# Loading the last image pair of a dilated convolution in ten pieces

## The chip, the cores and the metric

The kernel runs on one core of a Trainium2 chip. A core has five engines with their own instruction streams: PE multiplies matrices, DVE, ACT and POOL work elementwise, and SP only issues transfers here. Data move between device memory and the on-chip buffer by 16 DMA engines, which all the issuing engines share. The metric is the device time of one launch in microseconds (us). Before the change the median of three runs is 126.34 us, with 126.18 and 126.83 as the lowest and the highest.

## The reference

A 3x3 convolution with dilation 2 over 16 images of 64 channels and 64x64 pixels, with 128 output channels, zero padding, all in f32:

```python
x_pad = np.pad(x, ((0, 0), (0, 0), (pad, pad), (pad, pad)), mode='constant')
for b, co, ci, kh, kw in ...:
    output[b, co] += weight[co, ci, kh, kw] * x_pad[b, ci, kh*2:kh*2+h, kw*2:kw*2+w]
```

The input is 16.8 MB and the output 33.6 MB, so most of what moves is output.

## The kernel before

Images are taken in eight pairs. The two images' 64 channels each fill the 128 partitions of a tile `x16[pb]` (f16, 128 x 64 rows x 64 columns), so partition p below 64 is channel p of the first image, and the others are the second image. Pair 0 is loaded as f32 by SP (L75) and cast on chip. Pairs 1 to 7 are loaded by `load` (L81), issued by POOL, with the cast from f32 to f16 done on the way; each such load was one transfer of 128 partitions with 64 rows, 2 MB read and 1 MB written.

For each pair, POOL adds rows two apart into a tile `s16[pb]` (`prepare`, L141), in two parts, rows 0 to 36 and rows 36 to 64. PE then computes, for each of four row groups u of a pair, three accumulations in PSUM (`phase`, L186): one on the sums and two on differences of weights, on the even and the odd rows. ACT copies the first from PSUM (L204), DVE adds it to the other two and writes the output tile `o` (L209). The tile `o` has three buffers (128 partitions, 2 images, 64 rows, f32, 4 MB), so pair pb writes into the one whose store was issued for pair pb - 3.

The order is written out by hand; each engine executes its instructions in the order of the program. Loads of pairs 1 to 4 are issued at the beginning. The load of pair pb + 2 is issued by POOL in group u = 1 of pair pb, ahead of `prepare(pb + 1, 0, 36)` (L195 to L199); the load of pair 7 so stands in pair 5. There are six buffers for `x16`. Stores are issued by SP when a pair's last addition is done (L221): one of 4 MB for pairs 0 to 4, two of 2 MB for pairs 5 and 6 (L224), and four of 1 MB for pair 7, two after half of its rows.

Every transfer signals a semaphore when it has landed. Transfers issued by POOL use eight semaphores in turn, and those of SP another eight. An issue that comes to a semaphore again first waits until the transfer that used it before has landed.

Of the kernel before, what the change touches and what calls it, by code (L numbers as in the profile page):

```python
# [10 lines left out]
def kernel(  # L11
# [7 lines left out]
    nc = tc.nc  # L19

    B, CI, H, W = x.shape
# [5 lines left out]
    P = 128  # L27
    f32 = mybir.dt.float32
    f16 = mybir.dt.float16
    NP = B // 2  # L30
# [18 lines left out]
    wpool = ctx.enter_context(tc.tile_pool(name="wpool", bufs=1))  # L49
    x16pool = ctx.enter_context(tc.tile_pool(name="x16pool", bufs=6))  # L50
# [9 lines left out]
    x_pair = x.rearrange("(nb two) c h w -> nb (two c) h w", two=2)  # L60
# [5 lines left out]
    x16 = {}  # L66
# [11 lines left out]
    def load(pb, cuts):  # L78
        x16[pb] = x16pool.tile([P, H, W], f16, tag="x16", name=f"x16_{pb}")
        for lo, hi in zip(cuts, cuts[1:]):  # L80
            nc.gpsimd.dma_start(out=x16[pb][:, lo:hi], in_=x_pair[pb, :, lo:hi])  # L81

    AHEAD = 5

# [15 lines left out]
    for name, a in (("w21", 2), ("w01", 0)):  # L100
        for u in range(2):
            eng = nc.vector if name == "w21" else nc.gpsimd
            eng.tensor_sub(  # L103
                out=w16[:, SLOT[name] * KW : (SLOT[name] + 1) * KW, u, :],
                in0=w32k[:, a * KW : (a + 1) * KW, :],
                in1=w32k[:, KW : 2 * KW, :],
            )

            if name == "w01" and u == 0:
                load(1, [0, H])  # L110

    w_sb = wpool.tile([P, NS * KW, CO], f16, name="w_sb")
    for n, name in enumerate(("w1", "w21", "w0", "w01", "w2")):
        ps = cpool.tile([P, 2, NB], f32, tag="ps", name=f"wt{n}")
        k0 = SLOT[name] * KW
        for j in range(KW):
            nc.tensor.matmul(  # L117
                out=ps[:, 0, j * CO : (j + 1) * CO],
# [16 lines left out]
    def prepare(pb, lo, hi):  # L135
        if pb not in s16:
            s16[pb] = sumpool.tile([P, 2 * NQ, W], f16, tag="s16", name=f"s16_{pb}")
        src = (x16[pb] if pb else x32).rearrange("p (q e r) w -> p q e (r w)", e=2, r=2)
        dst = s16[pb].rearrange("p (q r) w -> p q (r w)", r=2)
        q0, q1 = lo // 4, hi // 4  # L140
        nc.gpsimd.tensor_add(  # L141
            out=dst[:, q0:q1], in0=src[:, q0:q1, 0, :], in1=src[:, q0:q1, 1, :]
        )

    prepare(0, 0, 20)
    for pb in range(2, AHEAD):
        load(pb, [0, H])
# [33 lines left out]
    def phase(pb, u, terms):  # L181

        ps = cpool.tile([CO, 2, NB], f32, tag="ps", name="ps")
        for pair in zip(*(conv(pb, hb, ps[:, hb], u, terms) for hb in range(2))):
            for m in pair:
                nc.tensor.matmul(**m)  # L186
        return ps

    BOTH = NP - 3
    for pb in range(NP):  # L190
        o = opool.tile([P, 2, H, W], f32, tag="o", name=f"o{pb}")
        ov = o.rearrange("p b (q e r) w -> p b q e (r w)", e=2, r=2)
        for u in range(NU):

            if u == 1 and AHEAD <= pb + 2 < NP:  # L195
                load(pb + 2, [0, H])
            if pb + 1 < NP:
                if u == 1:
                    prepare(pb + 1, 0, 36)  # L199
                elif u == 2:  # L200
                    prepare(pb + 1, 36, H)

            s32 = spool.tile([P, 2, NB], f32, tag="s32", name="s32")
            nc.scalar.copy(out=s32, in_=phase(pb, u, [("w1", 2, 0)]))  # L204
            for e, terms in enumerate(
                ([("w21", 1, 0), ("w0", 1, -1)], [("w01", 0, 0), ("w2", 0, 1)])
            ):
                ps = phase(pb, u, terms)
                nc.vector.tensor_add(  # L209
                    out=ov[:, :, u * UQ : (u + 1) * UQ, e, :],  # L210
                    in0=ps.rearrange("p b (q c) -> p b q c", c=QW),
                    in1=s32.rearrange("p b (q c) -> p b q c", c=QW),
                )

            step = NU // 2 if pb == NP - 1 else NU
            if (u + 1) % step == 0:
                fl = slice((u + 1 - step) * 4 * UQ, (u + 1) * 4 * UQ)
                if pb < BOTH:  # L220
                    nc.sync.dma_start(out=out_pair[pb], in_=o)  # L221
                else:
                    for hb in range(2):
                        nc.sync.dma_start(out=out[2 * pb + hb, :, fl], in_=o[:, hb, fl])  # L224
# [35 lines left out]
```

## Time and profile before

| | |
|---|---|
| median of three runs | 126.34 us (126.18 to 126.83) |
| span of the profiled execution, first to last instruction | 124.3 us |
| own time of the profiled execution | not listed apart from the span; the runs' median lies 2.0 us above the span |
| PE busy | 105.2 us (85%) |
| DVE busy | 80.8 us (65%) |
| ACT busy | 39.6 us (32%) |
| POOL busy | 41.4 us (33%) |
| DMA: queue of SP (q1) | 2944 packets, 35.95 MB, 68.9% of 16 engines' span |
| DMA: queue of POOL (q0) | 1008 packets, 7.34 MB, 28.4% of 16 engines' span |
| granted TensorE clock | 0.965 of full speed on the mean |

Shares are of the span. The megabytes are those written; POOL's loads read twice as many. A DMA share is the time that packets took, as a share of 16 engines. An average over the span hides that stages differ, so the slices and windows are read beside it: they give the busy time of each engine in each stretch. PE's time is modelled; a busy PE need not be PE at its peak.

### The profile page before, as it was taken

How to read it: one execution, taken by the hardware profiler on the slowest of the kernel's cores; microseconds unless marked ns; L12 is line 12 of the kernel's file. 1: busy time of each engine (PE TensorE's matmuls, PEld its weight loads, DVE VectorE, ACT ScalarE, POOL GpSimd, SP SyncE). 2: the span in 40 equal slices, each digit the busy share in tenths (PEclk: the TensorE clock that was granted, in tenths of full speed). 3: DMA queues.
4: the chain of work that ended last, by engine and by line, in shares of the span. 5: the costliest groups of instructions: out<-in, count | busy, mean ns of one | idle time of the engine just before them, and what ended most of it. 6: DMA issues, size and time to landing. Idle time of an engine off the chain costs nothing.

```text
span 124.3 us, 2244 instructions
## 1 busy us (share of the span) xinstructions
PE 105.2 (85%) x981; PEld 55.7 (45%) x981; DVE 80.8 (65%) x71; ACT 39.6 (32%) x40; POOL 41.4 (33%) x33
## 2 busy tenths in 40 slices
PE   6357999999999999999999999999999999960000
PEld 2043555555555555555555555555555555520000
DVE  0470199787778777877769778777877787770000
ACT  4760823333333333333333333333332433320000
POOL 2859998794095009500930093000000000000000
PEclk9999999999999999999999999999999999999655
DMA  4999999999999999999999999999999999999991
GB/s 129 346 359 218 214 214 216 224 237 411 393 327 314 332 306 319 316 390 314 324 345 427 425 427 432 422 427 427 432 438 427 432 414 432 427 417 419 422 406 71
DMA packets 3961, 43.42 MB, mean 349 GB/s; under 512 B 368, under 2 KB 368, under 8 KB 624
## 3 DMA queue, kind: packets, MB, share of 16 engines
q1 hardware_dynamic: 2944, 35.95, 68.9%
q0 software_dynamic: 1008, 7.34, 28.4%
q8 instruction: 7, 0.11, 0.3%
q14 instruction: 2, 0.02, 0.0%
HBM read 17.07 MB, written 33.55 MB: 407 GB/s over the span
## 4 chain that ended last, share of the span: by engine, by line
PE 80%; DMA 5%; POOL 2%; DVE 1%; DVEq 1%; SPq 0%; issue 0%
PE ps L186 80%; DMA x<-in_x_dram 5%; POOL s L141 2%; DVE o L209 1%; DVEq L255 1%; SPq L64 0%; DVEq L209 0%
## 5 line engine op out<-in xcount | busy, mean ns | idle before, releaser
L209 DVE TENSOR_TENSOR o<-ps,s 128x1024 f32<-128x1024 f32 x64 | 76.7, 1223 | 25.9 <-PE ps L186 16.8
L186 PE MATMUL ps<-x,w_sb 64*128 64x496 f16 (+3 forms) x768 | 85.3, 368 | 0.0
L186 PEld LDWEIGHTS <-w_sb 64*128 64x128 f16 x960 | 53.4, 95 | 49.3 <-issue 3.7
L204 ACT COPY s<-ps 128x1024 f32<-128x1024 f32 x32 | 32.4, 1012 | 63.0 <-PE ps L186 63.0
L141 POOL TENSOR_TENSOR s<-x 128x1152 f16<-128x1152 f16 (+4 forms) x18 | 35.1, 1971 | 31.1 <-PE ps L186 28.3
L186 PE MATMUL ps<-s,w_sb 64*128 64x496 f16 (+1 forms) x192 | 26.5, 379 | 2.1 <-POOL s L141 2.1
L81 POOL DMA_DIRECT2D x<-in_x_dram x7 | 4.0, 579 | 0.0
L132 ACT CAST x<-x 128x1024 f16<-128x1024 f32 (+1 forms) x3 | 2.8, 973 | 3.4 <-DMA x<-in_x_dram 3.4
L93 PE MATMUL warm<-zero 128*128 128x512 f16 x6 | 2.7, 630 | 1.2 <-DVE zero L87 1.2
L117 PE MATMUL wt<-ident,w 128*128 128x128 f16 x15 | 1.8, 312 | 2.1 <-ACT w L99 2.1
L103 DVE TENSOR_TENSOR w<-w 128x192 f16<-128x192 f32 x2 | 1.5, 800 | 2.5 <-DMA w<-in_weight_dram 2.5
L117 PEld LDWEIGHTS <-w 128*128 128x128 f16 x15 | 1.5, 146 | 3.0 <-ACT w L99 3.0
L99 ACT CAST w<-w 128x576 f16<-128x576 f32 x2 | 2.3, 1222 | 1.6 <-DMA w<-in_weight_dram 1.6
L103 POOL TENSOR_TENSOR w<-w 128x192 f16<-128x192 f32 x2 | 1.9, 951 | 2.4 <-DMA w<-in_weight_dram 2.4
L126 DVE CAST w_sb<-wt 128x384 f16<-128x384 f32 x3 | 1.6, 552 | 1.4 <-PE wt L117 1.4
L93 PEld LDWEIGHTS <-zero 128*128 128x128 f16 x6 | 0.7, 138 | 2.3 <-DVE zero L87 1.2
L99 ACT ACT_TABLE_LOAD x1 | 1.3, 1283 | 0.7 <-PEq L241 0.7
L128 ACT CAST w_sb<-wt 128x384 f16<-128x384 f32 x2 | 1.0, 478 | 1.1 <-PE wt L117 1.1
L130 DVE CAST x<-x 128x1280 f16<-128x1280 f32 x1 | 0.8, 826 | 0.5 <-DMA x<-in_x_dram 0.5
L87 DVE MEMSET zero<- 128x256 uint32 x1 | 0.3, 272 | 0.9 <-PEq L241 0.9
masks.py:199 POOL TENSOR_SCALAR_AFFINE_SELECT ident<-ident 128x128 f16<-128x128 f16 x1 | 0.3, 292 | 0.1
masks.py:197 POOL MEMSET ident<- 128x128 f16 x1 | 0.2, 204 | 0.3 <-POOLq L241 0.3
(4 smaller groups left out, 0.4 us busy)
## 6 DMA issues: line engine op xcount, KB each, us to landing
out_dram<-o SPq DMA_DIRECT2D x5, 4096.0 KB, 21.6
out_dram<-o SPq DMA_DIRECT2D x4, 2048.0 KB, 12.4
x<-in_x_dram POOLq DMA_DIRECT2D x7, 1024.0 KB, 16.0
out_dram<-o SPq DMA_DIRECT2D x4, 1024.0 KB, 10.6
x<-in_x_dram SPq DMA_DIRECT2D x1, 1152.0 KB, 6.5
x<-in_x_dram SPq DMA_DIRECT2D x1, 896.0 KB, 10.6
w<-in_weight_dram SPq DMA_DIRECT2D x1, 288.0 KB, 2.9
```

Of the source, the lines that this page charges most:

```text
L81: nc.gpsimd.dma_start(out=x16[pb][:, lo:hi], in_=x_pair[pb, :, lo:hi])
L93: nc.tensor.matmul(out=warm[:, 0], lhsT=zero[:, 0:P], rhs=zero, start=True, stop=True)
L99: nc.scalar.copy(out=w16[:, 0:NK, u, :], in_=w32k)
L103: eng.tensor_sub(out=w16[:, SLOT[name] * KW : (SLOT[name] + 1) * KW, u, :], in0=w32k[:, a * KW : (a + 1) * KW, :], in1=w32k[:, KW : 2 * KW ...
L117: nc.tensor.matmul(out=ps[:, 0, j * CO : (j + 1) * CO], lhsT=w16[:, k0 + j, :, :].rearrange("o t i -> o (t i)"), rhs=ident, start=True, st ...
L126: nc.vector.tensor_copy(out=dst, in_=ps[:, 0, 0 : KW * CO])
L132: nc.scalar.copy(out=x16[0][:, lo:hi], in_=x32[:, lo:hi])
L141: nc.gpsimd.tensor_add(out=dst[:, q0:q1], in0=src[:, q0:q1, 0, :], in1=src[:, q0:q1, 1, :])
L186: nc.tensor.matmul(**m)
L204: nc.scalar.copy(out=s32, in_=phase(pb, u, [("w1", 2, 0)]))
L209: nc.vector.tensor_add(out=ov[:, :, u * UQ : (u + 1) * UQ, e, :], in0=ps.rearrange("p b (q c) -> p b q c", c=QW), in1=s32.rearrange("p b ( ...
L255: with _tile.TileContext(nc) as tc:
```

## The change

The load of pair 7 is replaced by a function of its own, which issues ten loads in place of one: partitions 0 to 111 with all 64 rows; partitions 112 to 127 with rows 0 to 37; and rows 38 to 63 of these 16 partitions by eight loads of two partitions each. After them two small reads are issued, of three partitions with one row and of four partitions with two rows, into tiles of their own that nothing else reads. The other pairs are loaded as before. The rows and values that arrive in `x16[7]` are the same.

```diff
+    def load_uneven(pb):
+        x16[pb] = x16pool.tile([P, H, W], f16, tag="x16", name=f"x16_{pb}")
+        cut, p1 = H - 26, P - 16
+        parts = [(0, p1, 0, H), (p1, P, 0, cut)]
+        parts += [(p, p + 2, cut, H) for p in range(p1, P, 2)]
+        for p0, p2, lo, hi in parts:
+            nc.gpsimd.dma_start(
+                out=x16[pb][p0:p2, lo:hi], in_=x_pair[pb, p0:p2, lo:hi]
+            )
+        for n, row in ((3, 0), (4, 1)):
+            side = wpool.tile([P, (1 + row) * W], f32, name=f"side{n}")
+            nc.gpsimd.dma_start(
+                out=side[0:n].rearrange("p (h w) -> p h w", w=W),
+                in_=x_pair[pb, 0:n, 0 : 1 + row],
+            )
...
             if u == 1 and AHEAD <= pb + 2 < NP:
-                load(pb + 2, [0, H])
+                if pb + 3 == NP:
+                    load_uneven(pb + 2)
+                else:
+                    load(pb + 2, [0, H])
```

Further on, "the 112 partitions", "the 16 partitions" and "the two-partition loads" are the ten loads in the order of issue.

## The prediction

> **What bounds the kernel now.** I read the page first, then the time line of Pool, the waits, and last the table of windows, finely cut at the end. The page's slices and queues:
>
> ```profile
> PE   6357999999999999999999999999999999960000
> DMA  4999999999999999999999999999999999999991
> GB/s 129 346 359 218 214 214 216 224 237 411 393 327 314 332 306 319 316 390 314 324 345 427 425 427 432 422 427 427 432 438 427 432 414 432 427 417 419 422 406 71
> DMA packets 3961, 43.42 MB, mean 349 GB/s; under 512 B 368, under 2 KB 368, under 8 KB 624
> q1 hardware_dynamic: 2944, 35.95, 68.9%
> q0 software_dynamic: 1008, 7.34, 28.4%
> ```
>
> PE is full from slice 4 to slice 36, but the last four slices have no matmul and a DMA row still at 9. The DMA row is full from the second slice on. The low rates early are loads: the GB/s counts what is written (f16) while twice as much is read (f32), so 216 GB/s there is the same load on the engines as 430 GB/s of stores. The chain on the page (PE 80%) does not see this; it ends with the last DVE addition, 12 us before the span does. What comes after is only stores, and they were queued already:
>
> ```profile
> SPq L255 <- DMA out_dram<-o: 9.2, 4, 2.4
> DMA to landing us min/median/max: 8.9/9.9/10.9
> ```
>
> The second line is for the two stores issued at 112.0 and 112.4. Each is 1 MB and holds the 16 engines 2.5 us at 427 GB/s; the first landed after 8.9 us, so about 6 us of older stores stood ahead of it, less the way to memory and back. The end is therefore the moment when the slowest of the 16 DMA engines has worked off all that was ever given to it. The windows of the end show that they do not finish together (last two columns: mean share of the 16 that is busy, GB/s):
>
> ```profile
> 119.00:120.00 1.00, 0.00 (x0) 0.00 (x0) 0.00 (x0) 0.00 (x0) 0.00 (x0) 0.50 1.07 451
> 120.50:121.00 0.50, 0.00 (x0) 0.00 (x0) 0.00 (x0) 0.00 (x0) 0.00 (x0) 0.50 0.85 360
> 121.00:121.50 0.50, 0.00 (x0) 0.00 (x0) 0.00 (x0) 0.00 (x0) 0.00 (x0) 0.50 0.66 279
> 121.50:122.00 0.50, 0.00 (x0) 0.00 (x0) 0.00 (x0) 0.00 (x0) 0.00 (x0) 0.50 0.35 147
> 122.00:122.50 0.50, 0.00 (x0) 0.00 (x0) 0.00 (x0) 0.00 (x0) 0.00 (x0) 0.50 0.16 66
> 122.50:123.00 0.50, 0.00 (x0) 0.00 (x0) 0.00 (x0) 0.00 (x0) 0.00 (x0) 0.50 0.04 16
> ```
>
> Times 16, about 14 engines are at work before 121.0, 11 in the next half microsecond, then 6, 3, and under one. So some four engines are done by 121.0 (the earliest a little after 120.5), the other twelve stop one after another between 121.0 and 122.9, with their middle near 121.9. An engine that gets more work than before moves the end as soon as it passes 122.9; work taken from the others can only bring forward what the slowest one had.
>
> **The change part by part.** Everything outside the eighth pair's load keeps its order on all five engines; Pool has 12 DMA issues where it had one.
>
> *Bytes.* All rows of the pair are still read once. The 1008 packets of queue 0 are 7 x (128 + 16): one packet for each partition and one short completion packet for each engine, none cut finer (16 for each of the 23 DMAs also gives the 368 under 512 B). So 112 partitions are 7 packets on each engine, 16 partitions one each, and a load of two partitions is two packets and can lie on two engines at most.
>
> *Price of a packet.* In the windows where loads run alone:
>
> ```profile
> 10.00:15.00 5.00, 5.00 (x36) 2.41 (x36) 0.00 (x0) 2.69 (x3) 5.00 (x7) 1.00 1.02 216
> 15.00:20.00 5.00, 5.00 (x50) 2.73 (x48) 4.72 (x5) 2.02 (x2) 4.49 (x3) 1.00 1.06 221
> 20.00:25.00 5.00, 5.00 (x53) 2.68 (x50) 4.25 (x4) 1.23 (x2) 4.20 (x3) 1.00 1.03 215
> ```
>
> the mean is 217 GB/s, 13.6 for each engine; a partition writes 8192 bytes and so takes 0.604 us, one row of 64 takes 9.4 ns, 26 rows 0.245 us, 38 rows 0.36 us.
>
> *Who gets them.* Before, every engine had 8 x 0.604 = 4.83 us of this load. Now every engine has 7 x 0.604 + 0.36 = 4.59 us, and the sixteen 26-row packets come on top. If each two-partition load is dealt anew from the first engine, as the 128 partitions are, all eight land on the same two engines: these get 4.59 + 8 x 0.245 = 6.55 us (+1.72), the other fourteen lose 0.245. If successive loads go on to the next two engines, the eight cover all sixteen and nothing moves. The trace of before has no load of fewer than 128 partitions, so both are open; the bounds are 0 and +1.72 us on two engines. I take the upper one, because nothing in the trace shows a place that is carried from one load to the next, and every load in it starts evenly.
> On this the Trainium skill (DMA: Bandwidth & Descriptors, section "Why a DMA increments its semaphore by 16 and not by 1") states both: a software-issued copy whose size gives fewer than 16 engines takes consecutive ones from a round-robin cursor, yet some direct copies were measured to be dealt over 16 with ⌈partitions/16⌉ each, which for two partitions means the first two engines. By the first the sum would be +0.2 us, by the second it is the one below; no run here shows it yet.
>
> *Completions and marks.* Eleven more loads are eleven more completion packets on each engine. Their price: stores of 4 MB and more run at 437, 429 and 429 GB/s (70 to 85 us), where a DMA ends every 9.8 us; those of 2 and 1 MB at 426, 413 and 434 (105 to 120 us), where one ends every 2.5 to 4.9 us. The 2% are at most 0.045 us for each end, so 0 to 0.5 us for eleven; I take 0.2 us, since the lower rate also has other gaps in it. The two marked reads (768 and 2048 bytes) are under 20 ns by the rate above.
> The Trainium skill (DMA: Bandwidth & Descriptors) speaks against the change: "Rules for kernel authors" says to coalesce small transfers, and "Anatomy of one DMA" gives each software DMA about 2.0 us of fixed cost. As engine time that would be 11 x 2.0 = 22 us; the three windows above, with loads back to back and the engines busy throughout, do not show it as engine time, so nothing of it is in the sum.
>
> *Pool.* Its time line around the load:
>
> ```profile
> 46.58 4.21 POOL L141 TENSOR_TENSOR s<-x 128x1152 f16<-128x1152 f16 x2 [7.65 <-PE ps L186]
> 50.73 0.57 POOL L81 DMA_DIRECT2D x<-in_x_dram  x1
> 58.95 4.21 POOL L141 TENSOR_TENSOR s<-x 128x1152 f16<-128x1152 f16 x2 [7.65 <-PE ps L186]
> ```
>
> One issue takes 0.58 us on the mean of seven, twelve take 7.0 us, within the 7.65 us that Pool idles. But the software loads use eight semaphores in turn: in Pool's order the sixth two-partition load waits for pair 6's load, and the last two wait until the 112 and the 16 partitions have landed. The whole load landed 16.0 us after its issue, at 66.7; so Pool stands until about 66.5, and behind it `prepare(6)` starts near 68.5 instead of 58.95 and ends near 73. PE reads that sum first at 85.74 (start of pair 6 in PE's time line): 12 us of cover. `prepare(7)` begins at 73 instead of 71.31, its second half at 75.5 with the last small loads landed some 5 us before; PE needs it at 98.1. Cost 0; without that cover, each microsecond past 85.7 would stall PE by one.
>
> *PE, DVE, SP.* The slot of output buffers is reused when a store has landed; DVE waited for that once, 1.2 us. On the two loaded engines stores land up to 1.9 us later, so the next wait may be 1 to 2 us and push PE's end by less. The 6 us of stores queued at 112 hide it: cost 0.
>
> *Sum.* The loaded pair: +1.72 + 0.2 = +1.92 us each; the rest −0.245 + 0.2 = −0.05. If the later of the two stood in the middle of the twelve, 121.9, it ends at 123.8, and the last packet moves from 122.9 to 123.8: +0.9 us. The profiled span is 124.3 and would be 125.2; the median of the runs, 126.34, lies 2.0 us above the span, all outside the DMA tail, so 127.2. Measurement of this kernel (126.18 to 126.83 in three runs) cannot tell much under 0.5%, 0.63 us, from no change.
>
> **The rivals.**
> 1. *Two-partition loads rotate over the engines.* Nothing is moved, only completions are added: 126.34 + 0.2 = 126.5. For it: loads of 128 partitions, all that the trace has, would look the same with a moving start. Against it: no sign of a place kept.
> 2. *The fixed pair is early.* The other side of my forecast: if both engines are among the four that stop by 121.0, they end at 122.5 to 122.9, the rest at 122.85, and the end stays or comes 0.05 us earlier (0.25 if completions cost nothing): 126.1 to 126.4, not slower. It decides at a stop before of 121.0; up to 121.6 the loss stays under 0.63 us. By then about 7 of the 16 have stopped, so two drawn at random are both that early in 7/16 x 6/15 = 0.18 of cases; the first two engines may share a reason for being early, so I give more.
> 3. *Pool jams.* If the small loads' landing takes longer than I think, `prepare(6)` passes 85.7 and PE stalls; with PE late by more than the 6 us of queued stores the end follows. That needs Pool held past 87 us, 20 us more than I find: 128 to 130.
>
> **How the numbers follow.** Fixed pair, later member after 121.6: 0.55, own range 126.9 to 128.3 (a member at 122.9 plus 1.92, rounded up to the bound of completions). Fixed pair, early: 0.25. Rotating: 0.15. Pool: 0.03. Something that frees the slowest engine by over 0.63 us: 0.02; the relief itself cannot, being 0.245 us. The range 126.1 to 128.2 takes in all but the ends. Slower by over 0.5% gets 0.53 of the first case and the third rival, 0.56; within 0.5% the early pair, rotation and the rest of the first case, 0.41; faster 0.03.
>
> **What would show it.** Right: in the windows after 121 us, a share near 0.12 (two of 16) that lasts until the end, after the rest have stopped near where they did; Pool's last DMA issues after 64 us and `prepare(6)` near 68; PE without a wait at pair 6. Wrong: the same staircase as now at the same times (rotation, or an early pair, which a longer 0.85 plateau and a steeper end would tell), a wait of PE for Pool, or a DMA row below 9 before the end.

## The result, and the profile after

The median of six runs is 127.17 us (126.94 to 127.61), that of the kernel before on the same chip 126.19 us (126.14 to 126.83). The ratio is 1.0067, with a 95% interval of 1.0045 to 1.009: slower by 0.67%. The ratios in this document are estimated from all the fast runs, so they need not be the quotient of the two medians, which is 1.0077 here. The profiled execution took 127.02 us with a span of 124.7 us, against 124.3 us before.

The page of the kernel after, the lines that answer to those of before (DMA row by slices, rates, packets, queues), and the row of the new loads with their idle time:

```profile
DMA  4999999999999999999999999999999999999991
GB/s 135 365 349 215 221 210 218 213 252 412 420 302 326 305 310 326 328 418 305 307 333 426 422 419 414 447 426 426 415 436 426 436 407 426 431 423 418 428 384 45
DMA packets 4298, 43.42 MB, mean 348 GB/s; under 512 B 685, under 2 KB 689, under 8 KB 977
q1 hardware_dynamic: 2944, 35.95, 68.8%
q0 software_dynamic: 1344, 7.34, 28.4%
L89 POOL DMA_DIRECT2D x<-in_x_dram x10 | 5.1, 512 | 12.1 <-DMA x<-in_x_dram 12.1
```

The DMA row is as full as before and the same megabytes move; queue 0 has 336 packets more, and their time is still 28.4% of the engines' span. So the DMA engines remain what bounds the kernel. The windows of the end in the kernel after (last two columns: mean share of the 16 engines that is busy, GB/s):

```profile
121.00:121.50 0.50, 0.00 (x0) 0.00 (x0) 0.00 (x0) 0.00 (x0) 0.00 (x0) 0.50 0.62 262
121.50:122.00 0.50, 0.00 (x0) 0.00 (x0) 0.00 (x0) 0.00 (x0) 0.00 (x0) 0.50 0.47 197
122.00:122.50 0.50, 0.00 (x0) 0.00 (x0) 0.00 (x0) 0.00 (x0) 0.00 (x0) 0.50 0.20 82
122.50:123.00 0.50, 0.00 (x0) 0.00 (x0) 0.00 (x0) 0.00 (x0) 0.00 (x0) 0.50 0.12 49
123.00:123.50 0.50, 0.00 (x0) 0.00 (x0) 0.00 (x0) 0.00 (x0) 0.00 (x0) 0.50 0.04 16
```

A window counts a packet where it starts, so the last 0.04 is one packet of 0.31 us. By the packet records it starts at 123.18 and ends at 123.49, where the last packet of before ends at 122.90. Two engines work on past 122.5, and the other one stops at 123.0.

The packet records of the same trace also tell which engines these are, since each packet starts within some 20 ns of the end of the one before on its engine and can be followed. Two engines, and only these, carry nine short packets each of the eighth pair, one of 4864 bytes (38 rows in f16) and eight of 3328 (26 rows). One of the eight takes 266 ns, with 20 ns of overlap with the next: 0.246 us. One of this pair is the engine that stops at 123.5. The other stops by 122.5, though its chain is less certain, as some packets of different engines start within a nanosecond or two of each other. The engine that stops at 123.0 is not of the pair. It is an engine that is slower than the others in every trace: its last landing follows its last packet by 0.47 us, as in before, where it is the last to stop (0.46), while the other engines' last landings follow by 0.31 to 0.37. So the forecast share of 0.12 is there, but only one of the two engines behind it is of the pair, and that one ends at 123.5 and not at 123.8.

Pool's time line in the kernel after, between 45 and 90 us:

```profile
51.23 3.57 POOL L89 DMA_DIRECT2D x<-in_x_dram  x7
55.58 0.51 POOL L89 DMA_DIRECT2D x<-in_x_dram  x1 [0.78 <-DMA x<-in_x_dram]
66.28 0.50 POOL L89 DMA_DIRECT2D x<-in_x_dram  x1 [10.19 <-DMA x<-in_x_dram]
67.88 0.50 POOL L89 DMA_DIRECT2D x<-in_x_dram  x1 [1.10 <-DMA x<-in_x_dram]
69.11 0.51 POOL L94 DMA_DIRECT2D side<-in_x_dram  x1 [0.73 <-DMA x<-in_x_dram]
70.34 0.50 POOL L94 DMA_DIRECT2D side<-in_x_dram  x1 [0.72 <-DMA x<-in_x_dram]
70.86 6.54 POOL L157 TENSOR_TENSOR s<-x 128x1152 f16<-128x1152 f16 x3
78.19 1.88 POOL L157 TENSOR_TENSOR s<-x 128x896 f16<-128x896 f16 x1 [0.80 <-DMA x<-in_x_dram]
```

Seven issues go out at once, the eighth waits for the pair before, and the ninth stands 10.19 us until the 112 partitions have landed. `prepare(6)` starts at 70.86. PE does not feel it; the one wait of PE for Pool in the table of waits is that of the first pair, 2.0 us at the start:

```profile
PE ps L202 <- POOL s L157: 2.0, 1, 2.0
```

What the profile does not hold is more than half of the loss. Each run's time minus its own span is 1.77 us before (median of the 23 runs beside the first experiments; 1.73 to 1.85 over all calls) and 2.29 us after (2.24 to 2.32): +0.52 us outside the span, with no overlap of the two ranges. The median span is 124.9 us against 124.6 to 124.7 in the later calls: about +0.25 us inside it. In the call of the result, where the spans of the kernel before are not on record, the medians differ by 0.98 us, which leaves 0.46 us for the inside. Spans of one kernel differ by 1 us and more from run to run, so the size of the part inside is uncertain. Below, "above the span" means this difference, as a median of the runs.

### The profile page after: what moved, and what is told of

Same layout as the page of the kernel before. It is cut to its first block, busy times and chain, and to the rows that moved or that the text cites. A ratio compares the mean times of both kernels' runs of the same rounds, so it can differ in the third digit from the quotient of the medians.

```text
span 124.7 us, 2261 instructions
## 1 busy us (share of the span) xinstructions
PE 105.8 (85%) x981; PEld 54.8 (44%) x981; DVE 81.1 (65%) x71; ACT 39.5 (32%) x40; POOL 47.0 (38%) x44
## 3 DMA queue, kind: packets, MB, share of 16 engines
q0 software_dynamic: 1344, 7.34, 28.4%
## 4 chain that ended last, share of the span: by engine, by line
PE 81%; DMA 5%; POOL 2%; DVE 1%; DVEq 1%; SPq 0%; issue 0%
PE ps L202 81%; DMA x<-in_x_dram 5%; POOL s L157 2%; DVE o L228 1%; DVEq L274 1%; SPq L64 0%; DVEq L228 0%
## 5 line engine op out<-in xcount | busy, mean ns | idle before, releaser
L202 PE MATMUL ps<-x,w_sb 64*128 64x496 f16 (+3 forms) x768 | 86.4, 372 | 0.0
L89 POOL DMA_DIRECT2D x<-in_x_dram x10 | 5.1, 512 | 12.1 <-DMA x<-in_x_dram 12.1
L81 POOL DMA_DIRECT2D x<-in_x_dram x6 | 3.5, 586 | 0.0
L133 PE MATMUL wt<-ident,w 128*128 128x128 f16 x15 | 1.2, 219 | 2.2 <-ACT w L115 2.1
L133 PEld LDWEIGHTS <-w 128*128 128x128 f16 x15 | 0.9, 97 | 3.2 <-ACT w L115 3.0
L94 POOL DMA_DIRECT2D side<-in_x_dram x2 | 1.0, 502 | 1.5 <-DMA x<-in_x_dram 1.5
```

The lines of the kernel that those rows point to most:

```text
L89: nc.gpsimd.dma_start(out=x16[pb][p0:p2, lo:hi], in_=x_pair[pb, p0:p2, lo:hi])
L133: nc.tensor.matmul(out=ps[:, 0, j * CO : (j + 1) * CO], lhsT=w16[:, k0 + j, :, :].rearrange("o t i -> o (t i)"), rhs=ident, start=True, st ...
```

## The experiments

Each experiment was timed in five rounds beside the kernel before. "Pool's length" is the number of instructions in Pool's program: 55 before, 69 after (each trace holds one fewer).

**One part undone: the same number of loads, evenly dealt (e1_even).** The 26 rows come by eight loads of all 16 partitions with three or four rows each, so the number of loads stays and no pair of engines gets more.

```diff
-        parts += [(p, p + 2, cut, H) for p in range(p1, P, 2)]
+        rows = [cut, 42, 46, 49, 52, 55, 58, 61, H]
+        parts += [(p1, P, lo, hi) for lo, hi in zip(rows, rows[1:])]
```

> As many loads as in the change (ten and the two marked reads), but the last 26 rows of the 16 partitions come by eight loads of 16 partitions with 3 or 4 rows each, so no engine gets more than another. Theory A (two fixed engines carry 1.72 us more, and that sets the end): the loss of 0.98 us (126.19 to 127.17) goes, 126.2 to 126.4, and no pair of engines outlasts the rest. Theory B (the eleven more loads cost it, by their completion packets on every engine or by Pool's late prepare): 127.0 to 127.2.

Measured: 126.94 us against 126.47, ratio 1.0046 (1.0027 to 1.0066). The median span is 124.65 us against 124.7, so nothing is lost inside it; above the span it is 2.28 us, against 1.77 in the kernel before. The eleven further loads thus cost the DMA engines nothing that shows, and taking the pair's load away takes only about 0.25 us of the loss away, which six and twelve runs hardly tell from nothing. The time is near Theory B's, but the span does not hold it: something that both versions share costs 0.5 us outside the span.

**The pair alone, in two doses (e2_side3, e3_side6).** The kernel before, with three and with six whole two-partition reads of 64 rows behind Pool's last addition, where no engine waits for them. Each costs the two engines 0.604 us: +1.81 and +3.62 us.

```diff
                 elif u == 2:
                     prepare(pb + 1, 36, H)
+                elif u == 3 and pb + 2 == NP:
+                    side = wpool.tile([P, H, W], f16, name="side")
+                    for i in range(3):
+                        nc.gpsimd.dma_start(
+                            out=side[2 * i : 2 * i + 2], in_=x_pair[0, 2 * i : 2 * i + 2]
+                        )
```

> The kernel before, with three more loads of two partitions and 64 rows each (data not used), issued by Pool after its last addition. Pool's work and PE's inputs are untouched and only three loads are added. Theory A: 3 x 0.604 = 1.81 us more on two engines, as much as in the change; 127.0 to 127.3. Theory B: 3 of 11 loads' worth or nothing, 126.2 to 126.5.

> As the run with three side loads, but six: 3.62 us more on two engines. Theory A: from the point where the pair sets the end every microsecond on it counts in full, so 1.8 us above the run with three: 128.8 to 129.1. Theory B: twice the small loss of that run at most, under 126.8.

Measured: three reads 126.67 us, ratio 1.0018 (0.999 to 1.0046), median span 124.9 (+0.2), 1.77 us above the span. That is not clear of noise and less than the 127.0 to 127.3 of Theory A. Six reads 128.55 us, ratio 1.0176 (1.0144 to 1.0207), median span 126.4 (+1.7), 2.15 above the span. The windows of the end with six reads:

```profile
123.00:123.50 0.50, 0.00 (x0) 0.00 (x0) 0.00 (x0) 0.00 (x0) 0.00 (x0) 0.50 0.12 49
123.50:124.00 0.50, 0.00 (x0) 0.00 (x0) 0.00 (x0) 0.00 (x0) 0.00 (x0) 0.50 0.15 66
124.00:124.50 0.50, 0.00 (x0) 0.00 (x0) 0.00 (x0) 0.00 (x0) 0.00 (x0) 0.50 0.08 33
124.50:125.00 0.50, 0.00 (x0) 0.00 (x0) 0.00 (x0) 0.00 (x0) 0.00 (x0) 0.50 0.08 33
```

By the packet records the two engines that carry the reads, six each, stop at 124.43 and 125.16, and all others have stopped by 123.22. Two-partition reads all go to the same two engines; if they went round, six of them would have put 0.604 us on each of twelve engines and this tail would not be there. The larger dose also measures where the pair stands without it: 124.43 and 125.16 less 3.62 us are 120.8 and 121.5. In the kernel after, 122.5 and 123.5 less 1.72 us give 120.8 and 121.8. The later of the two thus has about 1.1 to 1.4 us of room to the slowest engine's 122.9, and some 0.3 more in a median run, whose span is that much longer than the traced one; so the first dose hardly shows.

**Many loads of a few bytes (e4_marks).** The kernel before with 14 one-row reads of 2 to 15 partitions in the same place.

```diff
+                elif u == 3 and pb + 2 == NP:
+                    for n in range(2, 16):
+                        side = wpool.tile([P, W], f32, name=f"side{n}")
+                        nc.gpsimd.dma_start(out=side[0:n], in_=x_pair[0, 0:n, 0])
```

> The kernel before, with fourteen reads of one row from 2 to 15 partitions (data not used), issued by Pool after its last addition. The number of marks that an engine's packets carry tells its place among the sixteen, and so where the first two engines end in the kernel before. Theory A: engines 0 and 1 end early enough that the relief does not matter and late enough that 1.72 us more passes the last one: between 121.2 and 122.0 in the profiled span; time 126.2 to 126.4. Theory B (each load costs 0.98/11 us): 14 loads give 127.4.

Measured: 127.38 us, ratio 1.0083 (1.0053 to 1.0114), median span 125.1 (+0.4), 2.28 above the span. This is the time that Theory B named, but most of it has another place: loads with almost no bytes cost the full 0.5 us outside the span again. They also served as marks: since the reads differ in their number of partitions, the packet records tell the engines apart. The engine that ends last (its last packet lands at 124.08, the next engine's at 122.91) carries 11 of the 14 marks, so it is the fifth, number 4 if the first is 0. It is the slow engine of the other traces.

By then the loads themselves were a suspect, and so was Pool's program, which is longer in after, e1, e3 and e4 than before.

**Pool's length without loads, and both at once (e5_pad14, e6_pad6, e7_side3_pad11).** The kernel before with 14, and with 6, memsets of one column behind Pool's last addition, and the three side reads of e2 with 11 memsets.

```diff
+                elif u == 3 and pb + 2 == NP:
+                    for i in range(14):
+                        nc.gpsimd.memset(side[:, i : i + 1], 0.0)
```

> The kernel before, with fourteen one-column memsets on Pool after its last addition: no load is added, Pool's program is as long as in the change (69 instructions, before 55). Theory C (half a microsecond of the change's loss lies outside the profiled span and comes from Pool's longer program): span as before, 124.6, time 0.45 to 0.6 us above the kernel before of this call, and an instruction packet of 8 KB after the end of the span. Theory D (it is the number of software loads that have to be closed): no loss, within 0.1 us.

> As the run with fourteen memsets, but six: Pool's program has 61 instructions, as with the six side loads, whose time lay 2.15 us above its span (before 1.77, the change 2.3). Theory C: 0.3 to 0.45 us above the kernel before, all outside the span. Theory D: within 0.1 us.

> The kernel before with the three side loads of two partitions (1.81 us more on two engines) and eleven memsets on Pool (69 instructions): the two suspected parts of the change's loss without its ten pieces. Theories A and C together: 0.2 us in the span and 0.5 us outside it, 0.7 to 1.0 us above the kernel before, the change's loss. Theory C alone: 0.5. Theory A alone: 0.2.

On Pool's time line in e5 the memsets are nothing, and they end 49 us before the span does:

```profile
74.87 0.54 POOL L205 MEMSET side<- 128x1 f32 x14
```

Measured: e5 127.08 us, ratio 1.0063 (1.0037 to 1.0089); e6 126.76, 1.0044 (1.0015 to 1.0073); e7 126.98, 1.0071 (1.0042 to 1.01). Without one more load or byte, 14 idle instructions cost nearly what the whole change costs. The time above the span is 2.28, 2.18 and 2.30 us, and the median spans (124.8, 124.6 and 124.7 against 124.6) are not clear of noise, so Theory D is out. e7 comes out no slower than e5, so it does not show the 0.2 us that Theory A adds to Theory C. In e5 it is not the end of the DMA work that moves; its windows at 122.0 and at 122.5 are those of before to 0.04:

```profile
122.00:122.50 0.50, 0.00 (x0) 0.00 (x0) 0.00 (x0) 0.00 (x0) 0.00 (x0) 0.50 0.12 49
122.50:123.00 0.50, 0.00 (x0) 0.00 (x0) 0.00 (x0) 0.00 (x0) 0.00 (x0) 0.50 0.04 16
```

**The ten pieces in a short program (e9_short), with its control (e10_before_short).** In e9 the kernel after is cut to 58 Pool instructions: the two marked reads go, the two `prepare` calls of a pair become one, the first pair's are joined into fewer, and Pool's subtraction of the weights (two instructions) moves to DVE. e10 is the kernel before with the same joining and moving, 45 instructions.

```diff
-            eng = nc.vector if name == "w21" else nc.gpsimd
+            eng = nc.vector
...
-    for lo, hi in zip(cuts0[1:], cuts0[2:]):
+    for lo, hi in ((20, 36), (36, H)):
         prepare(0, lo, hi)
...
                 if u == 1:
-                    prepare(pb + 1, 0, 36)
-                elif u == 2:
-                    prepare(pb + 1, 36, H)
+                    prepare(pb + 1, 0, H)
```

> The change's ten pieces without the two marked reads, with Pool's program cut back to 58 instructions by other means: its two additions of each pair from 1 to 7 and two of pair 0 merged, and the two subtractions of the weights given to DVE. The two engines still get 1.72 us more. Theory C: the time lies 1.77 us above the span again, not 2.29, and what is left of the change's loss is the 0.2 to 0.4 us in the span, measured against the kernel with the same merging and the eighth pair in one load. If the pieces themselves cost the half microsecond: 2.29 stays.

> The control for the merged versions: the kernel before with the same merging (45 Pool instructions) and the eighth pair in one load. Theory C: below the boundary the length does not matter; time 1.77 us above the span, and within 0.15 us of the kernel before. If the gain of the version with six loads came from the merging, this one has it too (0.45 us faster).

Measured: e9 127.92 us, ratio 1.0126 (1.0101 to 1.0151); e10 127.69, 1.0099 (1.0073 to 1.0124). Both are 1.3 to 1.5 us slower than the kernel before, for a reason of their own, which the traces point to and no run tested. The moved subtraction had held back a load on Pool. Pool's time lines, first of before, then of e10:

```profile
4.74 0.70 POOL L81 DMA_DIRECT2D x<-in_x_dram  x1
```

```profile
1.42 0.70 POOL L81 DMA_DIRECT2D x<-in_x_dram  x1
```

The load of pair 1 now competes with pair 0's own, and the chain that ended last shows it, in before and in e10:

```profile
1.17 6.48 DMA x<-in_x_dram
```

```profile
1.65 13.38 DMA x<-in_x_dram
```

So the two are compared with each other only: both stand at 1.78 us above the span, so the ten pieces in a program of 58 instructions lose nothing there. e9 is 0.25 us longer in its span (126.15 against 125.9), with ten pieces against one load. That agrees with the 0.25 us above, but with six runs each, spread over 0.9 and 1.0 us, it is not clear of noise.

**Uneven by design (e8_four, e11_four64, and e12_merged as control).** If some engines have room, work can be dealt to them on purpose. e8 deals by four partitions: 112 partitions whole, 24 rows of the last 16, and their last 40 rows by four loads of four partitions. Four engines get 4 x 40 x 9.4 ns = 1.51 us and all sixteen lose 0.38, so +1.13 us on the first four and −0.38 on twelve, the fifth among them. e11 takes the last 16 partitions by four whole loads of four (+1.81 on four, −0.60 on the others). Both join the `prepare` calls of pairs 1 to 7, which leaves Pool 56 and 54 instructions; e12 is the kernel before with that joining alone (48).

```diff
-        cut, p1 = H - 26, P - 16
+        cut, p1 = H - 40, P - 16
...
-        parts += [(p, p + 2, cut, H) for p in range(p1, P, 2)]
+        parts += [(p, p + 4, cut, H) for p in range(p1, P, 4)]
```

> An attempt at a faster version: the eighth pair by six loads, 112 partitions whole, 24 rows of the last 16, and their last 40 rows four partitions at a time; no marked reads; Pool's two additions of each pair from 1 to 7 merged into one, so that its program stays short (56 instructions). Engines 0 to 3 get 3 x 40 rows x 9.4 ns = 1.13 us more, the other twelve, with the slowest among them, 0.38 us less. Theory A with a slack of over 1.2 us on engines 0 to 3: 0.1 to 0.35 us faster than before. If engines 2 or 3 stand late: up to 0.8 us slower.

> The version with four-partition loads taken further: 112 partitions whole and the last 16 by four loads of four whole partitions. Engines 0 to 3 get 1.81 us more, the other twelve 0.60 us less than in the kernel before. With a slack of engines 0 and 1 of 1.4 to 1.9 us beside the slowest engine, their end passes the relieved rest: between the version with 40 rows and the kernel before, 126.0 to 126.6. If the four have more slack than that: 125.7.

> The kernel before with Pool's two additions of each pair from 1 to 7 merged into one (48 Pool instructions), nothing else: the control for the version with six loads of the eighth pair, which has this merging too. If that version's gain of 0.45 us comes from dealing the rows unevenly over the DMA engines: no change here, within 0.15 us. If it comes from the merging: 0.3 to 0.5 us faster.

Measured: e8 125.91 us against 126.36, ratio 0.9965 (0.9937 to 0.9994); e11 126.93, 1.0039 (1.001 to 1.0069); e12 126.41 against 126.26, 0.999 (0.9965 to 1.0015). e8 beats both kernels, by 0.35% over the one before, and joining alone (e12, timed in another call) gives nothing that shows, so the gain is the dealing's. The windows of the end in e8:

```profile
121.00:121.50 0.50, 0.00 (x0) 0.00 (x0) 0.00 (x0) 0.00 (x0) 0.00 (x0) 0.50 0.74 311
121.50:122.00 0.50, 0.00 (x0) 0.00 (x0) 0.00 (x0) 0.00 (x0) 0.00 (x0) 0.50 0.24 98
122.00:122.50 0.50, 0.00 (x0) 0.00 (x0) 0.00 (x0) 0.00 (x0) 0.00 (x0) 0.50 0.23 98
122.50:123.00 0.50, 0.00 (x0) 0.00 (x0) 0.00 (x0) 0.00 (x0) 0.00 (x0) 0.50 0.00 0
```

No packet starts after 122.5. By the packet records the four engines stop at 122.0 to 122.7 and the fifth, relieved, at 122.7; the kernel before ends at 122.9. e11 overshoots, and comes out slower than the 126.0 to 126.6 that were expected: after 122.5 its shares are 0.19, 0.23, 0.15 and 0.04, and three of its four engines run on beyond 124.

Set side by side, all kernels sort by Pool's length:

| kernels | Pool's length | above the span, us | instruction packet after the span |
|---|---|---|---|
| e10, e12, e11, before, e8, e2, e9 | 45, 48, 54, 55, 56, 58, 58 | 1.77 to 1.80 | none |
| e3, e6 | 61 | 2.15, 2.18 | none |
| after, e1, e4, e5, e7 | 69 | 2.28 to 2.30 | one of 8 KB, 1.0 to 1.2 us after the span's end |

Loads, memsets and bytes are mixed in each row, and only the length separates the rows; e9 with ten pieces stands in the first. That Pool's length causes the step is shown by e5 and e6, which add nothing but idle instructions, and by e9. What the chip does in that time is not shown, nor on which side of the span it lies. The last column, from the packet records, suggests that instructions are fetched after the work has ended, but the kernels with 61 instructions lose 0.38 us with no such packet on record. This stays open.

## Why the prediction was right, and where it was not

The time came out at 127.17 us where 127.2 was forecast, but two terms missed, in opposite directions. Inside the span it forecast +0.9 us and 0.25 to 0.46 came (0.47 between the two profiled executions); outside it forecast nothing and 0.52 came. The mechanism inside the span was right, but that the sum hit to 0.03 us is luck.

- **What bounds the kernel.** Right. With six reads on the pair the span grew by 1.7 us at the DMA engines' end, and e8 gained by dealing alone.
- **Price of a packet.** Right: 0.246 us for 26 rows, forecast 0.245.
- **Who gets them.** Right: the upper of the two bounds. The pair is fixed by the packet records and by e3, and the rival of rotation is out. Of the two statements of the Trainium skill (DMA: Bandwidth & Descriptors, section "Why a DMA increments its semaphore by 16 and not by 1"), the trace agrees with the second, ⌈partitions/16⌉ partitions for each engine from the first one on; no load here showed a cursor.
- **Where the pair stands.** Nearly right. The middle of the twelve, 121.9, was taken for the later of the two; by the packet records it stands at 121.5 (e3) to 121.8 (after), and the earlier one at 120.8. So it passes the slowest engine, as forecast, and the last packet moves from 122.9 to 123.5, 0.6 us and not 0.9. Of the 0.3 between, 0.1 is the place and 0.2 the completions, the term after next. The rival of the early pair set its limit for a loss under 0.63 us at a stop of 121.6, which lies inside the range found. So inside the span the forecast and this rival were close, and with a constant time above the span the loss would have stayed under 0.63 us.
- **The sign that was looked for.** A share of 0.12 near the end was found, but by chance: one of its two engines is the slow fifth, which the forecast did not know of.
- **Completions.** Taken at 0.2 us, with 0 as the lower bound; e1 has all eleven loads, evenly dealt, and its span is 0.05 us shorter than that of before. Zero was right for these, as far as the scatter lets one see. e4's 14 loads came with +0.4 us in the span, and in its trace the fifth engine ends 1.17 us after the next. That need not be the loads: in the trace of e12, which adds none, the fifth stops 2.3 us after the next, at 124.7. It wanders from one execution to another, so no single trace gives the end to better than some tenths.
- **Pool.** Right in its order and its cost, off in time. `prepare(6)` started at 70.86 and not at 68.5, since the small loads landed one after another, 1.0 to 1.5 us apart, and not in a bunch, and since the two marked reads had to wait as well (0.73 and 0.72 us), which the text left out; the second half of `prepare(7)` still waited 0.80 us for the last of them at 78.19, where they were thought to have landed 5 us before. The cover of 12 us was large enough: PE had no wait, and pair 6 started at 86.24.
- **What lies above the span.** This is the step that was missing. The text set the 2.0 us between the profiled span and the median of the runs as a constant, "all outside the DMA tail". Each run's own difference is 1.77 us, the other 0.2 being that the span came from an execution quicker than the median; and it is no constant: it rises by 0.52 us when Pool's program grows from 55 to 69 instructions.

## What to carry to other kernels

Where the DMA engines bound a kernel, its end is the slowest one of sixteen, so look at the windows of the end before dealing a transfer: here POOL's loads of n partitions, n below 16, put their data on the first n engines, and giving the rows to engines that stop early gained 0.35%. Take the time above the span for each run as a number of its own and compare it too; a half per cent sat there, and no view of the profile's span could show it. When an edit adds instructions to an engine, a version with as many idle instructions tells its program's length from its work.

## What the runs showed of the hardware that was not expected

- The step in the time above the span with Pool's length: 1.77 to 1.80 us up to 58 instructions, 2.15 to 2.18 at 61, 2.28 to 2.30 at 69. The Trainium skill (Runtime: NRT & Kernel Launch, section "Instruction fetch mechanics") says that an engine's instructions are fetched in blocks of 16 KiB, and that crossing into the next is mostly hidden. The traces show instruction packets of 16 KB and of 8 KB; if the step is a fetch, it is not hidden here.
- In the packet records of every kernel, seven instruction packets of 16 KB lie in the run, each holding one DMA engine for 0.88 to 1.13 us, and two of 8 KB for 0.31. They may make a part of the staircase at the end; no run tested it.
- One engine takes mostly 630 to 670 ns for a 16 KB packet of a store where the others take 611 to 624; by e4's marks it is the fifth. It is the last to stop in before and the last to land in e1 (123.79, the next 123.06) and e4, and it is among the twelve that e8 relieved.
- A small software load takes two turns at each engine between the store's packets of 0.61 us, one for its data and one for its completion, so a row of them lands about 1.2 us apart in e4, however few their bytes. An engine without data in such a load gets a further packet of 4 bytes: in the kernel after, 425 packets of 4 bytes on queue 0 where the completions alone make 18 x 16 = 288, and the other 137 are 8 x 14 + 13 + 12, the engines that the ten reads of two, three and four partitions leave out.
